# First feed-forward block of a decoder layer: both token halves taken by quarters of tokens, with one buffer and one weight moved

## The chip, the core and the metric

The kernel runs on one core of a Trainium2 chip. A core has five engines with a queue of instructions each, taken in order: TensorE (PE, with its weight loads shown as PEld), VectorE (DVE), ScalarE (ACT), GpSimd (POOL) and SyncE (SP), which issues most transfers. An engine waits at the head of its queue until the semaphores of that instruction are set; nothing behind it passes. The metric is the device time of one execution in microseconds, median of several runs.

## The reference, cut to what matters

```python
h = x + merged @ w_out
hn = rms_norm(h, norm_ffn)
return h + (jax.nn.silu(hn @ w_gate) * (hn @ w_up)) @ w_down
```

All in float32, with 1024 tokens, 1024 channels and 2816 feed-forward (FF) channels. What lies before `merged` (attention, convolution, cross-attention) isn't touched by the change.

## The kernel before

A float32 product is made of three matmuls on split operands: each operand is kept as a high part (rounded by ScalarE, L131) and a low part (the remainder, by VectorE or GpSimd, L132); `mm3` (L146) does high by high, high by low, low by high. Where a large product is made of 2 by 2 blocks, it is done in seven products instead of eight, on sums of operands ("seven", with the operands' sums in `T`).

The stage of interest lies between the output projection and the loop over FF blocks. The output projection's last matmuls (L1304) go row tile by row tile, eight tiles of 128 tokens. When one is complete, `row_done` calls `scale_h`: the sum of squares (L1197), the root by ScalarE (L138), the reciprocal (L140), and the scaled row tile `t` by VectorE (L1200), taken from a pool of four buffers, `t4`. Two row tiles make a quarter of 256 tokens. `norm_h(tp)` turns a quarter: TensorE transposes it in eight 128x128 pieces per tile (L236), four PSUM banks in all, and each bank is split into a high and a low part of `xn`, the operand of the FF products. There are two token halves of 512; quarters 0 and 2 make half 0, quarters 1 and 3 make half 1. Quarters 1 and 3 also make the sums `T` of "seven", from their own turned values and the raw values of quarters 0 and 2. These raw values are kept by ScalarE (L1231): half of them in the `fz` pool, the other half in a buffer of the `stage` pool (tag `st`), which has two buffers and is otherwise the landing place of raw weights.

FF block 0 (128 FF channels) is done plainly by `plain` (L1170), since it has no partner: gate and up products over one half at a time, 48 matmuls per product pair and quarter. For half 0 it is cut into two parts, with `norm_h(2)` between; half 1 is done in one part after `norm_h(3)`. Blocks 1 to 21 follow in a loop: `pieces(f)` loads the raw gate and up weights (SP, L1362) into `stage`, GpSimd makes the four sums (L1367 and L128), and they are split; `seven(f)` has 84 matmuls of 512 columns. After each block the activations are stored (L1146, L1152).

The order in each queue isn't the order of the code: a scheduler places instructions by priority, which falls with the place in the code, and by when it thinks operands are ready; a tile waits for a buffer of its pool. Once placed, the queues are fixed.

Of the kernel before, what the change touches and what calls it, by code (L numbers as in the profile page):

```python
# [8 lines left out]
F32 = mybir.dt.float32  # L9
F32R = mybir.dt.float32r  # L10
BF16 = mybir.dt.bfloat16
AF = mybir.ActivationFunctionType
OP = mybir.AluOpType
# [4 lines left out]
P = 128  # L18
# [3 lines left out]
KT = D // P  # L22
# [17 lines left out]
def hybrid_layer_kernel(  # L40
# [4 lines left out]
    nc = tc.nc  # L45
    x, mem, out = x[0], mem[0], out[0]
    w_in, w_mem_kv, w_out = w_in[0], w_mem_kv[0], w_out[0]
    w_gate, w_up, w_down = w_gate[0], w_up[0], w_down[0]
# [5 lines left out]
    stage = ctx.enter_context(tc.tile_pool(name="stage", bufs=2))  # L54
# [12 lines left out]
    def nm(s):  # L67
        count[0] += 1
        return f"{s}_{count[0]}"

    def slab(shape, dt=F32R):
        return slabs.tile([P] + shape, dt, tag="slab", name=nm("slab"))
# [13 lines left out]
    def t4(shape, dt=F32):  # L86
        return t4p.tile([P] + shape, dt, tag="t4", name=nm("t4"))

    def t2(shape, dt=F32, p=P):
        return t2p.tile([p] + shape, dt, tag="t2", name=nm("t2"))  # L90
# [8 lines left out]
    def bank(shape, dt=F32, p=P, at=None):  # L99
        if at is None:  # L100
            turn[1] += 1
            at = order[turn[1] % len(order)]
        return psp[at].tile([p] + shape, dt, tag=f"ps{at}", name=nm("ps"))

    def fbank(shape, dt=F32, p=P):
        return pfp.tile([p] + shape, dt, tag="pf", name=nm("pf"))

    def anybank(shape, dt=F32, p=P):
        turn[2] += 1
        j = turn[2] % 8  # L110
        return fbank(shape, dt, p) if j == 7 else bank(shape, dt, p, order[j])
# [15 lines left out]
    def sub(eng, o, a, b):  # L127
        eng.tensor_tensor(o, a, b, op=OP.subtract)  # L128
# [16 lines left out]
    def mm(o, a, b, start, stop):  # L145
        m = nc.tensor.matmul(o, a, b, start=start, stop=stop)  # L146
        n = 1
        for d in o.shape[1:]:
            n *= d
        products.append((m.ins, n if a.dtype == F32R else 4 * n))  # L150
        return m

    def mm3(o, ah, al, bh, bl, start, stop):
        first = mm(o, ah, bh, start, False)
        mm(o, ah, bl, False, False)
        mm(o, al, bh, False, stop)
        return first
# [86 lines left out]
    def xn(hl, k, half, a=0, b=512):  # L244
        return XN[half][k // 2][:, hl, k % 2, a:b]
# [20 lines left out]
    def unit(src, shape, alloc=wslab, eng=None, load=False, after=None):  # L266
        if alloc is fslab:
            st = fstp.tile([P] + shape, F32, tag="fst", name=nm("fst"))
        else:
            st = stage.tile([P] + shape, F32, tag="st", name=nm("st"))  # L270
        ld = nc.sync.dma_start(st, src)
        w = alloc([2] + shape)
        m, _ = split(w[:, 0], w[:, 1], st, eng)
        if after is not None:
            follow(m, after, "weights' cast behind attention's")
        return (w, ld.ins) if load else w

    def col_unit(w, c0, n=P, alloc=wslab, eng=None, load=False):
        return unit(w[:, c0:c0 + n].rearrange("(k p) c -> p k c", p=P), [w.shape[0] // P, n], alloc, eng,
                    load)  # L280
# [114 lines left out]
    b = bank([2 * KT])  # L395
# [11 lines left out]
    for u in range(2):  # L407
        w_ = slab([2, 2, 512])
        m, _ = split(w_[:, 0], w_[:, 1], raw_w[u])
# [20 lines left out]
    b = bank([4, TAPS + 3])  # L430
# [5 lines left out]
    b = bank([2, 16])  # L436
# [33 lines left out]
    for ct in range(4):  # L470
# [6 lines left out]
        for half in range(2):  # L477
            pg = chan_proj(wag, half)
# [10 lines left out]
    st = stage.tile([P, KT, 24], F32, tag="st", name=nm("st"))  # L489
# [14 lines left out]
    b = bank([NT, 24])  # L504
# [83 lines left out]
    for hp in range(2):  # L588
# [7 lines left out]
        b = bank([2, 256])  # L596
# [419 lines left out]
    with low(FILL):  # L1016
# [3 lines left out]
        for n_, h_ in halves:  # L1020
            b_, d_ = (2, 0, 1)[n_ // KT], n_ % KT
            if h_ == 0:
                ws[n_] = col_unit(w_in, C_GM + b_ * D + d_ * P, alloc=fslab,
                                  eng=nc.vector if n_ < N_EARLY else nc.gpsimd)
            w = ws[n_]
            ps = fbank([512])
            for k in range(KT):
                first = mm3(ps, w[:, 0, k, :], w[:, 1, k, :], xn(0, k, h_), xn(1, k, h_), k == 0, k == KT - 1)
# [70 lines left out]
    for n_, (br, wt) in enumerate(branches):  # L1099
        ins = nxt  # L1100
        for dp in range(4):
            w = unit(wt[0, :, dp * 256:(dp + 1) * 256].rearrange("(k p) c -> p k c", p=P), [4, 256],
                     alloc=anyslab if n_ else fslab if dp < 2 else wslab,
                     after=wcasts[-3] if n_ == 0 and dp > 1 else None)
# [4 lines left out]
            for d_ in (2 * dp, 2 * dp + 1):  # L1109
# [6 lines left out]
                for half in range(2):  # L1116
# [7 lines left out]
                    a = acc[dp][:, d_ % 2, half * 512:(half + 1) * 512]  # L1124
# [20 lines left out]
    def emit_act(f, half, a):  # L1145
        nc.sync.dma_start(ad[f][:, half * 512:(half + 1) * 512], a)  # L1146

    def left_low(f, a0, a1):

        s_ = t2([512])  # L1150
        sub(nc.gpsimd, s_, a0, a1)
        nc.sync.dma_start(ads[2, f], s_)  # L1152
# [14 lines left out]
    def gate_up(f):  # L1167
        return [col_unit(w, f * P, alloc=anyslab) for w in (w_gate, w_up)]

    def plain(f, half, w, parts=1, between=None):  # L1170
        pg, pu = (anybank([512]) for _ in range(2))
        for q in range(parts):
            a, b = q * 512 // parts, (q + 1) * 512 // parts
            if q:
                between()
            for o, w_ in ((pg, w[0]), (pu, w[1])):
                for k in range(KT):
                    mm3(o[:, a:b], w_[:, 0, k, :], w_[:, 1, k, :], xn(0, k, half, a, b), xn(1, k, half, a, b), k == 0,
                        k == KT - 1)
        s_ = t2([512])  # L1180
        nc.scalar.activation(s_, pg, AF.Silu)
        nc.vector.tensor_tensor(s_, pu, s_, op=OP.mult)
        emit_act(f, half, s_)
        return s_

    T = [[None] * 2 for _ in range(4)]
    raw, held, last = [None, None], [[], []], []

    def sb_fz():
        return fzp.tile([P, 2, 256], F32, tag="fz", name=nm("fz"))  # L1190
# [11 lines left out]
    def norm_h(tp, at=(None, None)):  # L1202


        half, q = tp % 2, tp // 2
        c = slice(q * 256, (q + 1) * 256)
        if q == 0:
            for kp in range(4):
                XN[half][kp] = slab([2, 2, 512])

        rows_at = []

        def turned(kp):
            b = turned_pair(js[tp], kp, at=at[kp % 2])
            rows_at.append(split(XN[half][kp][:, 0, :, c], XN[half][kp][:, 1, :, c], b))
            return b

        def keep(n, j, v, c=c):
            if T[n][j] is None:
                T[n][j] = slab([2, 2, 512])  # L1220
            two = split(T[n][j][:, 0, :, c], T[n][j][:, 1, :, c], v)
            if last:
                for pair_ in last:
                    for m, behind in zip(two, pair_):
                        tc.add_manual_dep(m.ins, behind.ins.name, ORDER, reason="sums' parts behind the rows'")

        if half == 0:
            raw[0] = [sb_fz() for _ in range(2)]
            raw[1] = stage.tile([P, 2, 2, 256], F32, tag="st", name=nm("st"))
            for kp in range(4):  # L1230
                nc.scalar.copy(raw[0][kp] if kp < 2 else raw[1][:, kp - 2], turned(kp))  # L1231
            return
        if q == 1:
            rows = [turned(kp) for kp in range(4)]
            last.extend(rows_at)
            for f_ in held[0]:
                f_()
            held[0].clear()
        for j in range(2):
            r0, r1 = (rows[j], rows[j + 2]) if q == 1 else (turned(j), turned(j + 2))  # L1240
            l0, l1 = raw[0][j], raw[1][:, j]
            d0, d1, d2 = (t2([2, 256]) for _ in range(3))
            sub(nc.vector, d0, r0, l0)
            sub(nc.vector, d1, r1, d0)
            eng = nc.vector if q == 1 else nc.gpsimd
            sub(eng, d2, d1, l0)
            sub(eng, l1, l1, d1)
            keep(0, j, d0)
            later = [lambda n=n, j=j, v=v: keep(n, j, v) for n, v in ((1, d1), (2, d2))]
            held[0] += later  # L1250
            held[1].append(lambda j=j, v=l1: keep(3, j, v))
            if q == 1:
                for f_ in held[0] + held[1][j::2]:
                    f_()
                held[0].clear()
# [75 lines left out]
    w0 = [col_unit(w_gate, 0)]  # L1331
# [8 lines left out]
    for q in range(2):  # L1340
        for j in (2 * q, 2 * q + 1):
            out_product(Y, s4, ws3, False, [(0, 1, True)], [j])
            row_done(j, 0)
            if q and j == 2:
                norm_h(1, (1, 0))
        if q:
            w0.append(col_unit(w_up, 0, eng=nc.gpsimd))
        for j in (2 * q, 2 * q + 1):
            out_product(X, plain_part(1, 1), ws4, False, [(1, 0, True)], [j])
            row_done(j, 1)  # L1350
            if j == 0:
                norm_h(0, (1, 1))
    a0 = plain(0, 0, w0, 2, lambda: norm_h(2, (1, 2)))
    norm_h(3)
    left_low(0, a0, plain(0, 1, w0))


    def pieces(f):
# [63 lines left out]
    w = pieces(1)  # L1422
    for f in range(1, FF // P):
        nxt = pieces(f + 1) if f + 1 < FF // P else None
        seven(f, *w)
        w = nxt
# [145 lines left out]
```

## Time and profile before

| | us |
|---|---|
| median of 3 runs | 1675.24 (1674.58 to 1677.42) |
| profiled execution, its time | 1675.84 |
| its span, first to last instruction | 1674.1 |
| PE busy in the span | 1632.1 (97%) |
| VectorE busy | 1100.9 (66%) |
| ScalarE busy | 745.8 (45%) |
| GpSimd busy | 669.8 (40%) |

The profile is of one execution. Times in its views run from the span's start. The stage of interest lies from about 1000 to 1080 us. A "releaser" is the instruction that the waiting engine's semaphore was set by last. The chain of waits follows the work back from the last instruction; a row there is start, length, and what ran.

### The profile page before, as it was taken

To read this page: it belongs to the slowest core of one execution; us is meant where nothing else is said; L and a number is where in the kernel's file an instruction comes from. 1 tells how busy PE (TensorE), PEld (TensorE's weight loads), DVE (VectorE), ACT (ScalarE), POOL (GpSimd) and SP (SyncE) were. 2 spreads that over 40 slices of the span, in tenths; PEclk is the share of its full clock that TensorE was granted. 3 is DMA by queue.
4 is the path that set the end of the run, shared out by engine and by line. 5 is a ranking of instruction groups with operands and counts; after the bars stand their busy time and mean duration, and the time that the engine had idled before them with its cause. 6 is when DMAs were issued, how large, how long until landed. Compare 5 with 4: busy or idle time off the path is not lost.

```text
span 1674.1 us, 22598 instructions
## 1 busy us (share of the span) xinstructions
PE 1632.1 (97%) x7904; PEld 1361.8 (81%) x7904; DVE 1100.9 (66%) x1828; ACT 745.8 (45%) x1371; POOL 669.8 (40%) x565
## 2 busy tenths in 40 slices
PE   7999999999999999999999999799999999999999
PEld 6887898777878888888788887688888888888887
DVE  6389989798666565656685867664545555466665
ACT  6311354442677676665664445333223223233332
POOL 0011004561466767656125331475566766400000
PEclk9999999999999999999999999899999999999999
DMA  8453446663355556448754432333234445893763
GB/s 286 159 172 113 149 143 177 206 200 108 108 159 166 162 153 179 134 128 266 245 178 151 164 113 95 101 120 101 88 112 139 145 154 186 283 387 122 238 227 120
DMA packets 252218, 277.87 MB, mean 166 GB/s; under 512 B 24309, under 2 KB 174117, under 8 KB 250567
## 3 DMA queue, kind: packets, MB, share of 16 engines
q1 hardware_dynamic: 245190, 263.83, 49.4%
q10 hardware_dynamic: 6912, 12.59, 2.0%
q8 instruction: 62, 1.02, 0.3%
q14 instruction: 54, 0.43, 0.1%
HBM read 191.43 MB, written 84.93 MB: 165 GB/s over the span
## 4 chain that ended last, share of the span: by engine, by line
PE 63%; DVE 6%; DMA 4%; POOL 3%; issue 3%; ACT 3%; SPq 0%; DVEq 0%; POOLq 0%; ACTq 0%
PE ps L146 31%; PE pf L146 14%; PE ps L1506 11%; PE ps L1304 3%; PE ps L965 1%; PE pf L1506 1%; DMA t<-zd 1%; DVE slab L132 1%; POOL slab L1130 1%; DMA fst<-in_w_mem_out_dram 1%; POOL slab L666 1%; DMA wd<-wsl 1%; DVE slab L467 1%; PE pf L1304 0%; DVE t L1129 0%
## 5 line engine op out<-in xcount | busy, mean ns | idle before, releaser
L146 PE MATMUL ps<-slab,wsl 128*128 128x512 f32 (+2 forms) x1664 | 362.3, 376 | 3.7 <-DVE slab L132 1.7
L146 PEld LDWEIGHTS ps<-slab,wsl 128*128 128x128 f32 x1664 | 296.8, 188 | 62.1 <-DVE slab L132 1.9
L146 PE MATMUL pf<-slab,fsl 128*128 128x512 f32 x1236 | 309.8, 394 | 3.8 <-ACT fz L1033 3.5
L146 PEld LDWEIGHTS pf<-slab,fsl 128*128 128x128 f32 x1236 | 226.9, 188 | 49.5 <-ACT fz L1033 6.1
L146 PE MATMUL ps<-slab,fsl 128*128 128x512 f32 x684 | 163.4, 394 | 6.9 <-ACT fsl L131 6.8
L467 DVE SCALAR_TENSOR_TENSOR slab<-slab,cw 128x1019 f32<-128x1019 f32 (+16 forms) x120 | 166.2, 1389 | 1.4
L1402 DVE TENSOR_TENSOR t<-ps,t 128x512 f32<-128x512 f32 x130 | 89.1, 688 | 114.5 <-PE ps L146 111.5
L146 PE MATMUL ps<-slab,slab 128*128 128x512 f32 (+1 forms) x628 | 152.8, 377 | 6.2 <-POOL slab L666 3.9
L146 PEld LDWEIGHTS ps<-slab,fsl 128*128 128x128 f32 x684 | 129.0, 190 | 35.3 <-ACT fsl L131 7.4
L146 PEld LDWEIGHTS ps<-slab,slab 128*128 128x128 f32 x628 | 112.4, 188 | 30.0 <-POOL slab L666 5.7
L1506 PE MATMUL ps<-wsl 128*128 128x512 f32 x495 | 118.9, 389 | 0.0
L1506 PEld LDWEIGHTS ps<-wsl 128*128 128x128 f32 x495 | 92.9, 188 | 19.3
L132 DVE TENSOR_TENSOR wsl<-st,wsl 128x1024 fp32r<-128x1024 f32 x57 | 84.6, 1485 | 33.5 <-ACT wsl L131 26.0
L146 PE MATMUL ps<-wsl,slab 128*128 128x512 f32 (+1 forms) x480 | 99.1, 353 | 0.4 <-DVE slab L228 0.3
L131 ACT CAST wsl<-st 128x1024 fp32r<-128x1024 f32 x61 | 63.9, 1050 | 77.7 <-PE ps L146 30.2
L146 PE MATMUL ps<-slab,qt 128*128 128x384 f32 (+6 forms) x400 | 93.8, 338 | 0.5 <-DVE sm L841 0.4
L146 PE MATMUL ps<-t,slab 128*128 128x256 f32 (+1 forms) x404 | 88.5, 319 | 1.5 <-DVE t L132 1.1
L146 PEld LDWEIGHTS ps<-wsl,slab 128*128 128x128 f32 x480 | 77.6, 192 | 12.1 <-DVE slab L228 0.5
L131 ACT CAST wsl<-t 128x1024 fp32r<-128x1024 f32 x43 | 45.3, 1054 | 89.8 <-POOL t L128 36.5
L1415 POOL TENSOR_TENSOR t<-t,t 128x512 f32<-128x512 f32 x21 | 40.0, 1907 | 112.3 <-DVE t L1402 42.0
L1506 PE MATMUL ps<-fsl 128*128 128x512 f32 x330 | 80.2, 389 | 0.0
L1130 POOL TENSOR_TENSOR slab<-slab,t 128x512 f32<-128x512 f32 x32 | 47.8, 1512 | 80.9 <-DVE t L1129 80.9
(256 smaller groups left out, 2938.1 us busy)
## 6 DMA issues: line engine op xcount, KB each, us to landing
t<-in_w_down_dram SPq DMA_DIRECT2D x70, 256.0 KB, 3.7
fst<-in_w_in_dram SPq DMA_DIRECT2D x24, 512.0 KB, 4.3
zd<-fz ACTq DMA_DIRECT2D x48, 256.0 KB, 2.4
slab<-wd SPq DMA_DIRECT2D x24, 512.0 KB, 4.6
t<-zd SPq DMA_DIRECT2D x24, 512.0 KB, 3.4
st<-in_w_gate_dram SPq DMA_DIRECT2D x22, 512.0 KB, 3.7
st<-in_w_up_dram SPq DMA_DIRECT2D x22, 512.0 KB, 4.4
ad<-t SPq DMA_DIRECT2D x44, 256.0 KB, 3.1
```

The lines of the kernel that those rows point to most:

```text
L131: m = nc.scalar.copy(hi, src)
L132: return m, (eng or nc.vector).tensor_tensor(lo, src, hi.bitcast(F32), op=OP.subtract)
L146: m = nc.tensor.matmul(o, a, b, start=start, stop=stop)
L467: return nc.vector.scalar_tensor_tensor(acc[:, s:], u[:, :S - s], cw[:, ct, 30 - s:31 - s], acc[:, s:], op0=OP.mult, op1=OP.add)
L666: part = nc.gpsimd.tensor_tensor(PT[:, 1, mb], PT[:, 1, mb].bitcast(F32), PT[:, 0, mb].bitcast(F32), op=OP.subtract)
L965: nc.tensor.transpose(b[:, j - j0, h, :], tiles[h][:, j * P:(j + 1) * P], ident)
L1130: nc.gpsimd.tensor_tensor(a, a, z, op=OP.add)
L1304: nc.tensor.matmul(B[j], a_(ha, k, j), w[:, hb, k % 2, :], start=start and k == 0 and n_ == 0, stop=stop and k == 3 and n_ == 2, skip_grou ...
L1402: nc.vector.tensor_tensor(o, a_, b_, op=OP.add)
L1415: nc.gpsimd.tensor_tensor(u4, u4, c22, op=OP.mult)
L1506: nc.tensor.matmul(B[t], a_, b_, start=start and k == 0 and j == 0, stop=k == FH - 1 and j == 2, skip_group_check=True)
```

## The change

Three edits.

1. FF block 0 is no longer done half by half. `plain` is gone; `first_part(n_, half, q)` does gate (n_ = 0) or up (n_ = 1) for one quarter of 256 tokens. The quarters 0 and 1 (both halves' first parts) come first, then the turning of quarter 2, its products, the activation of half 0, the turning of quarter 3 (now through PSUM pools 1 and 2), its products, the activation of half 1.
2. The raw half that lay in `stage` lies in a buffer of `t4`, the scaled row tiles' pool.
3. The low part of block 0's up weight is made by VectorE instead of GpSimd.

```diff
-            raw[0] = [sb_fz() for _ in range(2)]
-            raw[1] = stage.tile([P, 2, 2, 256], F32, tag="st", name=nm("st"))
+            raw[0], raw[1] = [sb_fz() for _ in range(2)], t4([2, 2, 256])
...
         if q:
-            w0.append(col_unit(w_up, 0, eng=nc.gpsimd))
+            w0.append(col_unit(w_up, 0))
...
-    a0 = plain(0, 0, w0, 2, lambda: norm_h(2, (1, 2)))
-    norm_h(3)
-    left_low(0, a0, plain(0, 1, w0))
+    first = [[anybank([512]) for _ in range(2)] for _ in range(2)]
+
+    def first_part(n_, half, q):
+        a, b = q * 256, (q + 1) * 256
+        w, o = w0[n_], first[half][n_]
+        for k in range(KT):
+            mm3(o[:, a:b], w[:, 0, k, :], w[:, 1, k, :], xn(0, k, half, a, b), xn(1, k, half, a, b), k == 0,
+                k == KT - 1)
+
+    def first_act(half):
+        s_ = t2([512])
+        nc.scalar.activation(s_, first[half][0], AF.Silu)
+        nc.vector.tensor_tensor(s_, first[half][1], s_, op=OP.mult)
+        emit_act(0, half, s_)
+        return s_
+
+    for n_ in range(2):
+        for half in range(2):
+            first_part(n_, half, 0)
+    norm_h(2, (1, 2))
+    for n_ in range(2):
+        first_part(n_, 0, 1)
+    a0 = first_act(0)
+    norm_h(3, (1, 2))
+    for n_ in range(2):
+        first_part(n_, 1, 1)
+    left_low(0, a0, first_act(1))
```

The queues move as follows. Lines after the change are numbered a little differently (L1200 is L1184, L1310 is L1293, L1338 is L1321, L1362 is L1369).

SyncE, around the stores of the finished rows `hd` (1 MB each). `st_9448` and `st_9679` are block 0's raw gate and up weights, `st_9999` and `st_10001` block 1's. Before:

```order
L271 DMA st_9448<-in_w_gate_dram 128x8x128
L1338 DMA hd<-slab_9062 128x2048
L1338 DMA hd<-slab_9063 128x2048
L1338 DMA hd<-slab_9064 128x2048
L271 DMA st_9679<-in_w_up_dram 128x8x128
L1338 DMA hd<-slab_9065 128x2048
L1146 DMA ad<-t_1681_9862 128x512
L1362 DMA st_9999<-in_w_gate_dram 128x8x128
L1146 DMA ad<-t_1700_9992 128x512
L1152 DMA ads<-t_1701_9996 128x512
L1362 DMA st_10001<-in_w_up_dram 128x8x128
```

And the same place now, where block 1's weights are `st_10047` and `st_10049`, and block 2's gate is `st_10070`:

```order
L271 DMA st_9448<-in_w_gate_dram 128x8x128
L271 DMA st_9679<-in_w_up_dram 128x8x128
L1369 DMA st_10047<-in_w_gate_dram 128x8x128
L1321 DMA hd<-slab_9062 128x2048
L1321 DMA hd<-slab_9063 128x2048
L1321 DMA hd<-slab_9064 128x2048
L1369 DMA st_10049<-in_w_up_dram 128x8x128
L1321 DMA hd<-slab_9065 128x2048
L1146 DMA ad<-t_1683_9912 128x512
L1369 DMA st_10070<-in_w_gate_dram 128x8x128
```

Block 0's up weight and block 1's gate weight moved ahead of three stores of rows, and block 1's up weight ahead of the first store of activations.

VectorE, where the first quarter's low parts (`slab_9520` to `slab_9523`) stand between the row tiles' sums and scalings (`t_1637` is the fourth scaled tile, `t_1641` the fifth). Before:

```order
L1200 SCALAR_TENSOR_TENSOR t_1637_9579<-slab_9063,sm_9577,gff 128x1024
L1310 TENSOR_TENSOR slab_9064<-ps_9076,slab_9064 128x512
L132 TENSOR_TENSOR slab_9520<-ps_9527,slab_9520 128x2x256
L132 TENSOR_TENSOR slab_9521<-ps_9535,slab_9521 128x2x256
L1197 TENSOR_TENSOR sm_9596<-sm_9058 128x1
L1310 TENSOR_TENSOR slab_9064<-ps_9077,slab_9064 128x512
L140 RECIPROCAL sm_9600<-sm_9598 128x1
```

And now (`wsl_9681` is block 0's up weight, `fsl_10057` block 1's gate weight):

```order
L132 TENSOR_TENSOR slab_9520<-ps_9527,slab_9520 128x2x256
L132 TENSOR_TENSOR slab_9521<-ps_9535,slab_9521 128x2x256
L140 RECIPROCAL sm_9600<-sm_9598 128x1
L1293 TENSOR_TENSOR slab_9064<-ps_9077,slab_9064 128x512
L132 TENSOR_TENSOR wsl_9681<-st_9679,wsl_9681 128x1024
L132 TENSOR_TENSOR fsl_10057<-st_10047,fsl_10057 128x1024
L1181 TENSOR_TENSOR sm_9670<-sm_9059 128x1
L1293 TENSOR_TENSOR slab_9065<-ps_9072,slab_9065 128x512
```

Two weights' low parts came into this place, and the fourth scaled tile left it (it now stands 14 rows behind the low part of `slab_9520`, just ahead of the fifth): `t4` has four buffers, and one of them is now held for the raw half.

TensorE, at the first products of FF block 0. `ps_9729` is the bank of gate for half 0 and `ps_9730` that of up; `pf_9731` is gate for half 1; `wsl_9450` and `wsl_9681` are the gate and up weights; `slab_9604` and on are half 1's operand. Before:

```order
L146 MATMUL ps_9729<-slab_9523,wsl_9450 128x256 x5
L236 MATMUL ps_9615<-identr,t_1622_9518 128x128
L236 MATMUL ps_9615<-identr,t_1637_9579 128x128
L236 MATMUL ps_9615<-identr,t_1622_9518 128x128
L236 MATMUL ps_9615<-identr,t_1637_9579 128x128
L146 MATMUL ps_9730<-slab_9520,wsl_9681 128x256 x2
L236 MATMUL ps_9782<-identr,t_1641_9602 128x128
```

And now:

```order
L146 MATMUL ps_9729<-slab_9520,wsl_9450 128x256 x6
L146 MATMUL ps_9729<-slab_9521,wsl_9450 128x256 x6
L146 MATMUL ps_9730<-slab_9520,wsl_9681 128x256 x6
L146 MATMUL ps_9729<-slab_9522,wsl_9450 128x256
L146 MATMUL ps_9730<-slab_9521,wsl_9681 128x256 x6
```

```order
L236 MATMUL ps_9840<-identr,t_1641_9602 128x128
L146 MATMUL pf_9731<-slab_9604,wsl_9450 128x256 x6
L236 MATMUL ps_9832<-identr,t_1641_9602 128x128
L146 MATMUL pf_9731<-slab_9605,wsl_9450 128x256
L236 MATMUL ps_9832<-identr,t_1661_9676 128x128
```

Gate and up of the first quarter now run side by side, and the products of the second quarter, which were 512 columns wide together with the fourth quarter at the end, stand between the turnings of the third.

More of the change, by code (lines that the diff above doesn't have):

```diff
@@ L1168, in gate_up @@
         return [col_unit(w, f * P, alloc=anyslab) for w in (w_gate, w_up)]
[L1170 to L1184, printed above, removed]
     T = [[None] * 2 for _ in range(4)]
```

## The prediction

> **What bounds the kernel now.** The page comes first: TensorE is busy 97% of the span, so only where it isn't can an edit of this kind gain.
>
> ```profile
> PE 1632.1 (97%) x7904; PEld 1361.8 (81%) x7904; DVE 1100.9 (66%) x1828; ACT 745.8 (45%) x1371; POOL 669.8 (40%) x565
> PE   7999999999999999999999999799999999999999
> PEclk9999999999999999999999999899999999999999
> ```
>
> Of the 40 slices only the first and the one at 1046 to 1088 us are below 9, the latter at a lower granted clock too. The windows of that stage show it closer (columns: stretch, its length, busy time of PE, PEld, DVE, ACT, POOL, granted clock, DMA share, GB/s):
>
> ```profile
> 1015.00:1020.00 5.00, 4.95 (x40) 4.60 (x38) 3.72 (x10) 3.54 (x9) 0.00 (x0) 1.00 0.48 190
> 1020.00:1025.00 5.00, 3.07 (x22) 2.69 (x23) 5.00 (x4) 2.98 (x6) 2.35 (x1) 1.00 0.13 52
> 1025.00:1030.00 5.00, 2.89 (x23) 2.48 (x23) 5.00 (x10) 1.65 (x3) 2.88 (x2) 1.00 0.00 0
> ...
> 1045.00:1050.00 5.00, 2.84 (x13) 2.02 (x11) 5.00 (x10) 3.38 (x6) 0.00 (x0) 1.00 0.00 0
> 1050.00:1055.00 5.00, 0.39 (x1) 0.40 (x2) 5.00 (x9) 2.61 (x5) 0.00 (x0) 0.67 0.36 105
> 1055.00:1060.00 5.00, 5.00 (x15) 3.68 (x15) 2.59 (x4) 0.59 (x2) 3.33 (x1) 0.64 0.23 84
> 1060.00:1065.00 5.00, 3.04 (x13) 1.87 (x12) 1.39 (x2) 1.10 (x2) 1.93 (x2) 1.00 0.44 126
> 1065.00:1070.00 5.00, 5.00 (x15) 3.89 (x16) 2.07 (x3) 3.01 (x4) 3.56 (x3) 0.66 0.38 110
> ```
>
> Two stretches have VectorE full and TensorE not (1020 to 1030, 1045 to 1055), and twice the clock falls to two thirds behind a pause. The waits of PE, for 990 to 1080 us, name the releasers:
>
> ```profile
> PE ps L146 <- ACT fsl L131: 6.8, 1, 6.8
> PE ps L146 <- DVE slab L132: 1.7, 1, 1.7
> PE ps L146 <- POOL wsl L132: 1.4, 1, 1.4
> PE pf L146 <- ACT u L131: 1.4, 1, 1.4
> PE ps L146 <- ACT wsl L131: 0.6, 1, 0.6
> PE pf L146 <- DVE u L132: 0.6, 1, 0.6
> PE ps L236 <- DVE t L128: 0.4, 1, 0.4
> ```
>
> They add up to 12.9 us. The longest ends with the cast of block 1's gate weight, which the timeline follows back to a load issued only at 1049.87, when the raw half had left its buffer of `stage`; the up weight came later still:
>
> ```profile
> 1049.87 0.38 SPq L1362 DMA_DIRECT2D st<-in_w_gate_dram  x1
> 1053.51 1.05 ACT L131 CAST fsl<-st 128x1024 fp32r<-128x1024 f32 x1
> 1054.61 7.64 PE L146 MATMUL ps<-slab,fsl 128*128 128x512 f32 x24 [6.77 <-ACT fsl L131]
> 1059.19 0.38 SPq L1362 DMA_DIRECT2D st<-in_w_up_dram  x1
> 1064.94 4.14 PE L146 MATMUL pf<-slab,u 128*128 128x512 f32 x10 [0.58 <-DVE u L132]
> 1068.92 5.68 PE L146 MATMUL ps<-slab,fsl 128*128 128x512 f32 x24
> ```
>
> **The bound of the gain.** The chain of waits (start, length, what) gives the prices of TensorE's work:
>
> ```profile
> 1028.90 3.13 PE ps L146 x24
> 1033.77 1.20 PE ps L236 x11
> 1034.97 2.98 PE pf L146 x13
> 1069.08 10.96 PE ps L146 x48
> ```
>
> A 256-column matmul costs 0.130 us, a transpose 0.109, a 512-column matmul 0.228. From 1015.4, where FF block 0 starts, to 1080.0, where block 1 ends (the last row: 1069.08 + 10.96), before runs 96 narrow and 48 wide matmuls, 40 transposes and block 1's 84 wide ones: 12.5 + 11.0 + 4.4 + 19.2 = 47.1 of 64.6 us. The other 17.5 are the 12.9 of waits and the slow clock: 24 matmuls took 7.64 for 5.5, and of the 12 on `u` the last 10 took 4.14 for 2.3, together 4.0.
>
> After the change half 1 is done in quarters: 48 wide matmuls become 96 narrow ones, 12.5 for 11.0, **+1.5 us**. Six transposes of the second quarter move from ahead of block 0 to behind its start, so it starts at 1014.9 with 46. In all 25.0 + 5.0 + 19.2 = 49.2 us: with no wait block 1 would end at 1064.1, a gain of 15.9.
>
> The Trainium skill, "TensorE: Matmul & The Clock Gate", under "Wait — 56ns, not 53.3ns?", gives the spacing of warm matmuls as columns by 2.4 GHz plus 2.5 ns, an estimate of 109 ns for 256 columns and 216 for 512, so that halving the columns would cost next to nothing and the gain be 1.4 us larger. The rows above have 130 ns, and the sum goes by them.
>
> **What goes.** The wait of 6.8 goes: block 1's gate weight now lands in the `stage` buffer that block 0's gate leaves, and its load stands ahead of the rows' stores. That buffer and the one for block 0's up weight come free with the first two of these rows; the others are the up weight's load before, and its cast:
>
> ```profile
> 991.07 2.39 POOL L132 TENSOR_TENSOR fsl<-st,fsl 128x1024 fp32r<-128x1024 f32 x1 [6.07 <-ACT fsl L131]
> 992.38 2.17 DVE L132 TENSOR_TENSOR wsl<-st,wsl 128x1024 fp32r<-128x1024 f32 x1 [0.44 <-ACT wsl L131]
> 1009.89 0.38 SPq L271 DMA_DIRECT2D st<-in_w_up_dram  x1
> 1019.44 1.05 ACT L131 CAST wsl<-st 128x1024 fp32r<-128x1024 f32 x1
> ```
>
> So the loads go out at 993.5 and 994.6 instead of 1009.9 and 1049.9. From issue to cast the slowest of the stage's loads took under 10 us (1009.89 to 1019.44, while rows were stored), so both lie ready by 1005. The 1.4 and 0.6 for block 0's up weight go too: its high part is cast at about 1008.2 (behind the casts of the first two banks), the low part by VectorE at about 1009.5, when TensorE still has the output projection. Gone with GpSimd's part is what it did to VectorE:
>
> ```profile
> 1012.96 2.48 DVE L1200 SCALAR_TENSOR_TENSOR t<-slab,sm,gff 128x1024 f32<-128x1024 f32 x2
> 1020.62 2.35 POOL L132 TENSOR_TENSOR wsl<-st,wsl 128x1024 fp32r<-128x1024 f32 x1 [27.16 <-ACT wsl L131]
> 1020.78 4.47 DVE L1200 SCALAR_TENSOR_TENSOR t<-slab,sm,gff 128x1024 f32<-128x1024 f32 x2
> ```
>
> Two scalings took 2.48 alone and 4.47 beside it: 2.0 us of VectorE's queue.
>
> **What stays, and what is new.** VectorE's queue sets the pace until about 1030. Its 128x512 operations follow at 0.60 (three in 1.87), scalings at 1.20:
>
> ```profile
> 1020.87 1.20 DVE t L1200
> 1026.97 1.87 DVE L132 TENSOR_TENSOR slab<-ps,slab 128x512 fp32r<-128x512 f32 x3
> 1018.93 0.02 issue
> ```
>
> Laid out by hand along the new queues: the two weights' low parts end at 1012.5 (the second waits for ScalarE's cast, which waits for the last output matmul on the old buffer, some 0.6 us; behind it stand row sums which TensorE needs only at 1018). The fourth and fifth scalings, late for want of a `t4` buffer, end at 1018.1 and 1019.3; TensorE meanwhile has 48 narrow matmuls of quarter 0, until 1021.0, so they cost nothing. Then it does the transposes of the second quarter, and four waits come, each on a row of VectorE's queue: the cast of the third bank, behind `t` of L128, 0.7; the cast of the first bank of quarter 2, 0.3; the PSUM bank that the next L128 frees behind two scalings and two low parts, 1.1 (VectorE 1026.85, TensorE 1025.8); the low part of `slab_9605`, two rows further, 0.7. From there TensorE has 60 narrow matmuls at a stretch, over 7 us, and VectorE goes ahead. The last scaling waits for a `t4` buffer until the last transposes of quarter 2 (1035.7), but 23 matmuls lie between those and its use, 3.0 us for 1.3.
>
> The second heap is the sums `T`: some 26 operations of VectorE (0.60 each) from 1044.4, with the four sums of block 1's weights by GpSimd beside them, which wait for `t4` buffers until quarter 3 is turned (1043.2). TensorE has 10 matmuls of block 1 and the rest of half 1 until 1050.5. The price of GpSimd beside VectorE shows in one row of before: 1.25 us of work took 3.33 beside VectorE's operations on SBUF operands.
>
> ```profile
> 1055.40 3.33 POOL L128 TENSOR_TENSOR t<-t,t 128x512 f32<-128x512 f32 x1 [21.76 <-DVE t L1182]
> ```
>
> I take it that the two alternate: VectorE loses about 3.2 us (2.6 times 1.25), and TensorE waits 1.6 at the first product on `slab_9629` and 0.5 for the bank of quarter 3, **2.1**. The ends are 0 (no collision) and 6.5 (VectorE keeps the lock while its operations follow each other, as in this row; rival 1). Beside that, some twenty hand-offs between engines at up to 0.05 (the row "issue"): 1.0.
>
> The Trainium skill, "SBUF — State Buffer", "SBUF: two separate sides", says that VectorE with two SBUF operands and GpSimd share a port pair under a lock that whoever starts first holds for a whole instruction. The rows at 1020.6 agree (the scaling ran 3.3 us); who is next when both queue, the page leaves open, and that is the 2.1 against 6.5.
>
> **Sum.** 15.9 − 0.7 − 0.3 − 1.1 − 0.7 − 2.1 − 1.0 = **10.0 us**. Behind block 1 the queues are the same but for names from block 5 on. Block 2's up weight stands on SP behind the last store of block 0's activations; by the same layout its low part ends at 1074.1 and is used at 1075.0, so it is hidden by a margin of 0.9. The profiled execution took 1675.84 for a span of 1674.1; less 10.0 that is 1665.8, and the median of the runs stands 0.6 below that execution: **1665.2**.
>
> **The rivals.**
> 1. *VectorE keeps the lock.* Then GpSimd's second and third sum come at 1045.7 and 1050.6 and the fourth after 1054, the casts of block 1's sums behind them; TensorE waits 2.5 and 3.4 instead of 1.6 and 0.5, and a pause of that kind halves the clock for some matmuls, 2.0 as at 1054.61. Gain 10.0 − 3.8 − 2.0 = 4.2: **1671.0**. For it: the row at 1055.40. Against: elsewhere its next operation waited in turn, as in the row below, 1.1 us longer than alone while a GpSimd sum ran. Chance 0.15.
>
> ```profile
> 1092.02 2.31 DVE L132 TENSOR_TENSOR slab<-t,slab 128x1024 fp32r<-128x1024 f32 x1
> ```
>
> 2. *No collision, or less.* GpSimd's four sums fit into VectorE's operations on PSUM: gain 12.1, and without hand-offs 13: **1662.2**. Chance 0.17.
> 3. *VectorE becomes the bound through the whole stage.* GpSimd has nine operations there; if each costs VectorE its full 1.25 and TensorE follows one to one, that is 11.3 instead of 3.2, a gain of 1.9: **1673.3**, no change. Against: four of the nine stand beside VectorE's reads of PSUM, where before shows them at their bare length. Chance 0.08.
> 4. *Slower: the weights' low parts at the head of VectorE's queue.* `fsl_10057` waits for its load ahead of the row sums and every scaling. It costs nothing up to an end at 1014.9 (1012.5 and 2.4 of slack), then one to one; the whole gain is gone when it ends at 1024.9, that is when the load lands after 1022. Behind the rows' stores at twice the 9.55 us that a load took there (landing 1029) it would be 6.6 late beyond that: **1681.8**. Against: the load is issued ahead of the stores. Chance 0.05.
>
> That the raw half's new place makes the rows wait (five tiles for four buffers) is in the sum; that the change doesn't do what it says would leave the gate weight's load at 1049.9, and the queue of SP excludes it.
>
> **How the numbers follow.** The forecast has 0.55. A measurement of this kernel can tell 0.2% (3.35 us) from no change, so faster is below 1671.9: 0.55 + 0.15 + 0.17 = 0.87; same 0.08; slower 0.05. The range reaches from rival 2 to rival 1, with half a microsecond to a whole on each side for the layout by hand: 1661.2 to 1671.5, which holds 0.85.
>
> **What would show it.** Windows of 1015 to 1080: PE near 5.00 from 1015 to 1023 and from 1030 to 1050, the two gaps at 1023 to 1028 and at about 1051, the granted clock at 1.00 throughout, block 2 from about 1070. The load of block 1's gate weight at 994 to 995. GpSimd's first operation in the stage only near 1027. Wrong would be: a wait of PE over 3 us, a clock below 0.9, low parts of weights on VectorE that start after 1015, or PE waiting for block 2's `wsl`.

## The result, and the profile after

| | before | after |
|---|---|---|
| median, us | 1676.33 (1674.58 to 1678.26, 4 runs) | 1664.10 (1662.73 to 1664.77, 4 runs) |
| ratio after to before, 95% interval | | 0.9926 [0.9909, 0.9943] |
| profiled execution, its time | 1675.84 | 1664.77 |
| its span | 1674.1 | 1663.0 |

The change makes the kernel 0.6 to 0.9% faster. The forecast was 1665.2, the time is 1664.1. The page of after has no slice below 9 behind the first, and 48 matmuls more, as two narrow ones take the place of one wide one:

```profile
PE 1630.5 (98%) x7952; PEld 1363.2 (82%) x7952; DVE 1103.2 (66%) x1829; ACT 746.5 (45%) x1371; POOL 669.7 (40%) x564
PE   7999999999999999999999999999999999999999
PEclk9999999999999999999999999999999999999999
```

The windows of the stage (columns as in the prediction: stretch, length, busy time of PE, PEld, DVE, ACT, POOL, granted clock, DMA share, GB/s):

```profile
1020.00:1025.00 5.00, 3.91 (x31) 3.44 (x30) 4.09 (x5) 3.52 (x7) 0.00 (x0) 1.00 0.01 2
1025.00:1030.00 5.00, 3.87 (x30) 3.45 (x30) 5.00 (x10) 1.98 (x4) 2.85 (x2) 1.00 0.00 0
...
1045.00:1050.00 5.00, 4.10 (x31) 3.48 (x29) 5.00 (x7) 3.85 (x7) 2.19 (x2) 1.00 0.29 84
1050.00:1055.00 5.00, 4.15 (x12) 3.00 (x13) 5.00 (x8) 2.39 (x4) 0.00 (x0) 0.73 0.08 24
1055.00:1060.00 5.00, 5.00 (x22) 4.13 (x21) 5.00 (x8) 2.04 (x4) 0.00 (x0) 0.93 0.00 0
```

The two gaps stand where they were forecast, at 1023 to 1028 and at 1050; TensorE does 3.9 of 5 us in the first where before had 3.0. What was not forecast is the clock: 0.73 and 0.93 behind the second gap. The waits of PE in 990 to 1085 us:

```profile
PE ps L146 <- DVE slab L132: 1.2, 1, 1.2
PE pf L146 <- ACT slab L131: 0.7, 1, 0.7
PE ps L236 <- DVE t L128: 0.7, 1, 0.7
PE ps L146 <- DVE t L128: 0.6, 1, 0.6
PE pf L146 <- DVE slab L132: 0.5, 1, 0.5
PE ps L146 <- ACT slab L131: 0.3, 1, 0.3
```

They are the six of the forecast, 4.0 us in all for 12.9 before, and none of them is for a weight. Of the loads, in SP's timeline (block 0's up weight, block 1's gate and up weight), the first two went out when it said:

```profile
992.76 0.38 SPq L271 DMA_DIRECT2D st<-in_w_up_dram  x1
993.84 0.37 SPq L1369 DMA_DIRECT2D st<-in_w_gate_dram  x1
1009.87 0.38 SPq L1369 DMA_DIRECT2D st<-in_w_up_dram  x1
```

Of the 11.1 us between the two spans, 0.7 had been won ahead of the stage: the six matmuls of the output projection that start at 985.62 in before start at 984.88 in after. The change doesn't touch what runs there, and in a second profile of after they start at 984.57, in a span of 1662.7: the lead is scatter. The stage itself gave 10.4, by the second profile 10.35.

### The profile page after: what moved, and what is told of

Read it like the earlier page. It is cut to its first block, busy times and chain, and to the rows that moved or that the text cites. A ratio compares the mean times of both kernels' runs of the same rounds, so it can differ in the third digit from the quotient of the medians.

```text
span 1663.0 us, 22705 instructions
## 1 busy us (share of the span) xinstructions
PE 1630.5 (98%) x7952; PEld 1363.2 (82%) x7952; DVE 1103.2 (66%) x1829; ACT 746.5 (45%) x1371; POOL 669.7 (40%) x564
## 4 chain that ended last, share of the span: by engine, by line
PE 71%; DVE 4%; POOL 2%; issue 2%; ACT 2%; DMA 1%; SPq 0%; DVEq 0%; POOLq 0%; ACTq 0%
PE ps L146 37%; PE pf L146 15%; PE ps L1513 11%; PE ps L1287 4%; PE ps L965 2%; PE pf L1513 1%; DVE slab L467 1%; POOL slab L666 1%; PE pf L1287 1%; POOL t L643 0%; ACT t L637 0%; DMA wd<-wsl 0%; POOL t L132 0%; PE ps L951 0%; DVE t L132 0%
## 5 line engine op out<-in xcount | busy, mean ns | idle before, releaser
L131 ACT CAST wsl<-st 128x1024 fp32r<-128x1024 f32 x61 | 64.0, 1050 | 75.7 <-PE ps L146 30.3
L131 ACT CAST wsl<-t 128x1024 fp32r<-128x1024 f32 x43 | 45.3, 1054 | 87.6 <-POOL t L128 28.7
```

What stands on the lines that cost most here:

```text
L131: m = nc.scalar.copy(hi, src)
```

## The experiments

### The three edits apart

Six kernels hold the other combinations of the three edits. The diffs are against the kernel before, and for those that take one edit back, against the kernel after.

**Edit 2 alone.**

```diff
-            raw[0] = [sb_fz() for _ in range(2)]
-            raw[1] = stage.tile([P, 2, 2, 256], F32, tag="st", name=nm("st"))
+            raw[0], raw[1] = [sb_fz() for _ in range(2)], t4([2, 2, 256])
```

> The kernel before with edit 2 alone (the raw half in a buffer of t4). Theory A, mine: the early load carries the gain. The gate load of block 1 goes out at 994 to 996, the wait of 6.8 us on its cast is gone, so are the waits on u (1.4 and 0.6), and most of the slow clock behind them; what is left is a pause at the sums T. Gain 7 to 11 us, 1665 to 1669. Theory B: the order by quarters carries it, since it gives TensorE work under VectorE's full stretches. Then this kernel gains less than 4: above 1672.

**Edit 3 alone.**

```diff
-            w0.append(col_unit(w_up, 0, eng=nc.gpsimd))
+            w0.append(col_unit(w_up, 0))
```

> The kernel before with edit 3 alone (the up weight's low part by VectorE). Theory A: the loads stay where they were (block 1's gate at about 1049), so that what TensorE wins at the first products it waits longer on that weight: gain 0 to 2 us, 1674 to 1676.5. Theory C: GpSimd beside VectorE's scalings is what held the stage up, and the gain is 4 us or more: below 1672.

**Edit 1 alone** (the kernel after, with the lines of edits 2 and 3 as before).

```diff
-            raw[0], raw[1] = [sb_fz() for _ in range(2)], t4([2, 2, 256])
+            raw[0] = [sb_fz() for _ in range(2)]
+            raw[1] = stage.tile([P, 2, 2, 256], F32, tag="st", name=nm("st"))
...
-            w0.append(col_unit(w_up, 0))
+            w0.append(col_unit(w_up, 0, eng=nc.gpsimd))
```

> The kernel after with edits 2 and 3 undone (order by quarters alone). Theory A: the gate load of block 1 is still issued at about 1049 and TensorE, which has done the second quarter's products by then, waits 6 to 9 us on its cast: gain 0 to 3, 1673 to 1676.5. Theory B: gain 6 or more, below 1670.

**Without edit 1** (the kernel before, with edits 2 and 3).

```diff
-    for n_ in range(2):
-        for half in range(2):
-            first_part(n_, half, 0)
...
+    a0 = plain(0, 0, w0, 2, lambda: norm_h(2, (1, 2)))
+    norm_h(3)
+    left_low(0, a0, plain(0, 1, w0))
```

> The kernel after with edit 1 undone: half 1 in wide products behind the fourth quarter, raw half in t4, up weight by VectorE. Theory A: the loads are early, 48 narrow matmuls fewer win 1.5 us, and the products missing between the turnings cost about as much in waits at VectorE's casts: 1663.5 to 1668. Theory B: the order was the main thing, and 6 us or more are lost against the kernel after: above 1670.

**Without edit 2.**

```diff
-            raw[0], raw[1] = [sb_fz() for _ in range(2)], t4([2, 2, 256])
+            raw[0] = [sb_fz() for _ in range(2)]
+            raw[1] = stage.tile([P, 2, 2, 256], F32, tag="st", name=nm("st"))
```

> The kernel after with edit 2 undone (raw half in the stage pool again). Theory A: block 1's gate load is issued only when that buffer is left, at about 1045 to 1050, TensorE waits 5 to 9 us for its cast, and a slow clock follows: 1671 to 1676. Theory B (the order by quarters carries the gain): below 1668.

**Without edit 3.**

```diff
-            w0.append(col_unit(w_up, 0))
+            w0.append(col_unit(w_up, 0, eng=nc.gpsimd))
```

> The kernel after with edit 3 undone (the up weight's low part by GpSimd). The loads are early, so GpSimd makes it at about 1008 to 1011, ahead of the scalings: theory A expects no difference, 1663.3 to 1665.3. Theory C (GpSimd's part was what held VectorE) expects 3 us or more, above 1667.

Measured, with the kernel after once more from a later run:

| edits | median, us | ratio to before, 95% interval |
|---|---|---|
| 1 | 1675.49 | 0.9998 [0.9990, 1.0007] |
| 3 | 1674.57 | 0.9991 [0.9982, 1.0000] |
| 1, 3 | 1675.51 | 1.0000 [0.9991, 1.0009] |
| 2 | 1665.33 | 0.9932 [0.9920, 0.9945] |
| 2, 3 | 1665.28 | 0.9935 [0.9923, 0.9948] |
| 1, 2 | 1664.59 | 0.9935 [0.9923, 0.9948] |
| 1, 2, 3 | 1664.10 | 0.9926 [0.9909, 0.9943] |
| 1, 2, 3 again | 1663.41 | 0.9931 [0.9918, 0.9945] |

Every kernel with edit 2 is 10 to 12 us faster; those without it lie within 0.1% of before. Edits 1 and 3 are worth nothing that these runs can measure, alone or beside edit 2; something like 1 us for edit 1 would be hidden in the scatter. Theory A (the early load carries the gain) had the time right in all six, B (the order by quarters does) and C (GpSimd's part does) in none where they were asked; without edit 1 the time is 1665.28, inside A's 1663.5 to 1668.

Why the order by quarters brings nothing shows in the timeline of edit 2 alone. These are a row of SP and two of PE:

```profile
994.78 0.37 SPq L1361 DMA_DIRECT2D st<-in_w_gate_dram  x1
```

```profile
1029.16 5.11 PE L146 MATMUL ps<-slab,wsl 128*128 128x256 f32 x24 [1.22 <-DVE slab L132]
...
1036.92 3.01 PE L146 MATMUL ps<-slab,fsl 128*128 128x512 f32 x12 [0.68 <-ACT t L1230]
```

With block 1's gate weight there early, the scheduler put 12 of block 1's own matmuls between the turnings. The kernel has work for TensorE's gaps from block 1 and needs none from the second quarter. It waits 4.4 us in the stage, after 4.0, and saves the 1.5 of the narrow matmuls. Most of what it saves went into the clock, which was slow here for two windows of 3.4 us and in after for one: the 24 narrow matmuls in the first row took 5.11 for the 3.13 of before. From the start of block 0 (1015.09) to the end of block 1 (1070.0, by the spans) it took 54.9 us, after 54.7.

Edit 3 alone shows the loads where they were and TensorE waiting at them. The first two rows are waits of PE, the others issues of block 1's weights:

```profile
PE ps L146 <- ACT fsl L131: 6.5, 2, 5.6
PE ps L146 <- DVE wsl L132: 1.0, 1, 1.0
```

```profile
1048.55 0.38 SPq L1362 DMA_DIRECT2D st<-in_w_gate_dram  x1
1057.86 0.38 SPq L1362 DMA_DIRECT2D st<-in_w_up_dram  x1
```

Block 0's up weight is late by its load, not by GpSimd: a wait of 1.0 stays, with VectorE as the releaser. And with edits 1 and 2 GpSimd does the part at 1008.93 in 2.41 us, ahead of the fourth scaling; VectorE starts it at 1008.63 in after. So it was the early load that took GpSimd's work out of VectorE's way, not the change of engine.

### Which of the two loads

In before the up weight of block 1 is loaded 9 us behind the gate weight. Two kernels separate the wait that the profile names (for the gate weight) from that load. The first fills the wait of 6.8 us with 28 matmuls, whose results the next product overwrites; the loads don't move.

```diff
-    def product(w, o):
+    def product(w, o, fill=0):
         ps = anybank([512])
+        for _ in range(fill):
+            m = nc.tensor.matmul(ps, w0[0][:, 0, 0, :], xn(0, 0, 0), start=True, stop=True)
...
-        nc.scalar.copy(p1, product(wt(A, 0), xb(0, 0)))
+        nc.scalar.copy(p1, product(wt(A, 0), xb(0, 0), 28 if f == 1 else 0))
```

> The kernel before with 28 matmuls more, whose results the product behind them overwrites, placed in the wait of 6.8 us for block 1's gate weight (28 x 0.228 = 6.4). Nothing else moves. Both theories expect the granted clock at 1.00 from 1048 to 1058 instead of 0.67 and 0.64. If the slow clock was a cost of its own there, block 1 ends 3.4 us earlier: 1672 to 1673. If the up weight's load (issued at 1059.19) bounds what follows, the won time turns into a longer wait on u (2.0 us before, then 4 to 5.5): 1674.5 to 1676.5.

PE's timeline (L1391 are the fillers) and two windows of it:

```profile
1047.79 6.51 PE L1391 MATMUL ps<-slab,wsl 128*128 128x512 f32 x28
...
1056.57 4.81 PE L146 MATMUL ps<-slab,fsl 128*128 128x512 f32 x20 [0.64 <-DVE fsl L132]
1063.75 0.82 PE L146 MATMUL pf<-slab,u 128*128 128x512 f32 x2 [2.37 <-ACT u L131]
```

```profile
1050.00:1055.00 5.00, 4.57 (x20) 3.49 (x20) 5.00 (x9) 2.50 (x5) 0.00 (x0) 1.00 0.37 105
1055.00:1060.00 5.00, 4.37 (x19) 3.28 (x19) 2.72 (x4) 1.31 (x3) 3.34 (x1) 1.00 0.21 78
```

The clock stays at 1.00 in both windows, and the time is 1676.30 (ratio 1.0003 [0.9994, 1.0012]). Part of the 2.1 us that the clock won went into a wait of 0.64 for the gate weight's low part, which the slow matmuls had covered; the 24 matmuls end at 1061.4, in before at 1062.2 (the first row below). What was won there went into the wait for the cast of `u`, 2.4 us for 1.4. Both waits on `u` together are 2.9 for 2.0, less than the 4 to 5.5 expected. The first product on `u` starts where it did in before (these rows are of before):

```profile
1057.46 4.78 PE L146 MATMUL ps<-slab,fsl 128*128 128x512 f32 x18
1063.63 0.73 PE L146 MATMUL pf<-slab,u 128*128 128x512 f32 x2 [1.38 <-ACT u L131]
```

It can't start earlier, since its load is issued at 1059.2 and the cast follows the landing. So the slow clock at 1051 to 1059 cost before nothing of its own. The second slow stretch, behind the wait for `u`, is there with the fillers too. One more window was slow in this profile, at 1023.28, and shorter waits behind it took that up: the last product of block 0 ends where it did in before.

The second kernel is after with block 1's up weight alone back behind the store of block 0's activations:

```diff
         for w in (w_gate, w_up):
...
+        if f == 1:
+            tc.add_manual_dep(m.ins, stored[0].ins.name, ORDER, reason="block 1's up weight behind block 0's stores")
```

> The kernel after, with block 1's up weight alone loaded where it was before, behind the store of block 0's difference of activations; the gate weight stays early. Theory A in the form that the fillers left of it (both loads are late in before, and the up weight's, the later one, sets when block 1 ends): TensorE does the 24 matmuls on the gate weight early, then waits for u until about 1064 to 1067 with 60 matmuls to go, and the gain is gone: 1672 to 1677. Theory A as forecast (the wait on the gate weight's cast is the main term): most of the gain stays, 1664 to 1669.

```profile
1059.55 0.38 SPq L1371 DMA_DIRECT2D st<-in_w_up_dram  x1
```

```profile
1050.91 3.00 PE L146 MATMUL ps<-slab,fsl 128*128 128x512 f32 x12 [0.45 <-DVE t L128]
1064.02 5.51 PE L146 MATMUL pf<-slab,u 128*128 128x512 f32 x12 [10.11 <-ACT u L131]
```

The time is 1674.35 us (0.9993 [0.9984, 1.0002]). With the gate weight early and the up weight late, the whole gain is gone: one wait of 10.1 us for `u`. So the later load sets the end of block 1. In before it stood behind the gate weight's load, which waited for the raw half's buffer, and behind the stores of block 0's activations in SP's queue; edit 2 moved both loads ahead of all that.

### The second gap

GpSimd's four sums of block 1's weights run beside VectorE's sums `T`. This kernel gives them the third `wsl` buffer, so that they needn't wait for `t4`, and queues them behind quarter 1's last subtraction:

```diff
-        s12, s34 = t4([2, 4, P]), t4([2, 4, P])
+        if f == 1:
+            both = wslab([2, 2, 4, P], F32)
+            s12, s34 = both[:, 0], both[:, 1]
+        else:
+            s12, s34 = t4([2, 4, P]), t4([2, 4, P])
...
+        if f == 1:
+            for i_ in (m, m2):
+                tc.add_manual_dep(i_.ins, raws[1].ins.name, ORDER, reason="block 1's sums behind quarter 1's")
```

> The kernel after, with block 1's four sums by GpSimd in the third wsl buffer instead of two of t4, queued behind quarter 1's last subtraction: they run at about 1034 to 1040, where VectorE has pauses, instead of 1041 to 1047 beside the sums T. If the alternation of GpSimd and VectorE (some 2.7 us of VectorE's queue) makes the two pauses of TensorE at the sums T (1.2 and 0.6) and these the slow clock (0.73 and 0.93, 1.9 us): all of it goes, the clock is 1.00 throughout, 1660 to 1661.5. Rival: VectorE's own 26 operations bound TensorE there, and the pauses stay within half a microsecond: 1663 to 1664.5.

1662.77 us (0.9923 [0.9910, 0.9935]). The two rows below are the same two operations of VectorE, in after beside GpSimd's sums and here without them:

```profile
1042.60 3.52 DVE L132 TENSOR_TENSOR slab<-t,slab 128x512 fp32r<-128x512 f32 x2
```

```profile
1043.66 1.28 DVE L132 TENSOR_TENSOR slab<-t,slab 128x512 fp32r<-128x512 f32 x2
```

GpSimd cost VectorE 2.2 us at that place, and 0.5 at the next two operations of this kind (1.79 for 1.29, at 1046.64 in after). Both pauses at the sums are gone, and the clock is 1.00 through the stage, as the first theory has it. But two new waits came, for a copy of the raw half and for a low part, since the cast and the low part of the first sum now stand ahead of them:

```profile
1038.85 0.66 PE L236 MATMUL ps<-identr,t 128*128 128x128 f32 x4 [0.86 <-ACT t L1214]
...
1040.33 0.86 PE L146 MATMUL pf<-slab,wsl 128*128 128x256 f32 x5 [0.48 <-DVE slab L132]
```

The time lies between the two theories, and its interval overlaps that of after.

Two more kernels go on from there. One also moves the scaling of quarter 3's first row tile behind quarter 1's subtractions:

```diff
+        if t == 6:
+            tc.add_manual_dep(m.ins, subs[-1].ins.name, ORDER, reason="quarter 3's first row behind quarter 1's sums")
```

> As the run with the early sums, and the scaling of the first row tile of quarter 3 (1.2 us) queued behind quarter 1's subtractions, ahead of nothing that TensorE waits for. If VectorE's queue makes the pauses at 1023 to 1028, those for t of L128 (0.7) and for the low part of slab_9605 (0.5) go or shrink: a further 0.6 to 1.1 us, 1659 to 1661. Rival: the pauses there are hand-offs that the scaling doesn't matter to, no difference from the run with the early sums.

1662.96 us. The waits of the first gap shrank as expected, from 0.6 to 0.3 (for `t`) and from 0.5 to 0.24 (for the low part). They came back at the next scaling, which now stood beside GpSimd's sums, and the time is the rival's, that of the run with the early sums:

```profile
1034.90 2.26 DVE L1184 SCALAR_TENSOR_TENSOR t<-slab,sm,gff 128x1024 f32<-128x1024 f32 x1 [2.46 <-PE ps L236]
```

It took 1.29 in after, and TensorE waited 0.6 for it. The other puts the first sum's cast and low part behind the rows that they had delayed:

```diff
+        if f == 1:
+            for i_, behind in ((m[0], kept[-1]), (m[1], last[0][1])):
+                tc.add_manual_dep(i_.ins, behind.ins.name, ORDER, reason="block 1's first sum behind quarter 3's rows")
```

> The run with the early sums, and the cast of block 1's first sum queued on ScalarE behind the last copy of the raw half, its low part on VectorE behind quarter 3's first low part. If the two new pauses of that run (0.86 for the copy, 0.48 for the low part) came from those two rows standing ahead, they go: 1661 to 1662, the clock 1.00 or one window down. Rival: the low part in its new place delays the sums T and the pauses come back there: 1662.5 to 1664.

1663.90 us (0.9929 [0.9916, 0.9941]). The wait of 0.86 for the copy went, but one of 0.43 for a cast came behind it; that of 0.48 became 0.22, and new ones of 0.2 and 0.3 came further on. The sum of the waits went from 3.5 to 3.3. The rival had the time. Beside it ran the kernel after, unchanged:

> The kernel after once more, beside the run with the held sum and on the same chip: 1663.5 to 1664.8. If the clock falls by whole windows of 3.41 us on a grid that has nothing to do with the program, the stage shows a drop at another place than the first profile, or none, with the same waits.

1663.41 us, 0.1 below what was expected, with the same six waits as in the first profile. The clock was expected to fall at another place or not at all; it fell at nearly the same place, from 1051.97 to 1055.38 for 1052.26 to 1055.67. None of the three variants can be told from after. What is left of the stage are short waits for VectorE and ScalarE, and in these three runs moving one row made another one late.

## Why the prediction was right, point by point

**The bound and the sum.** From the start of block 0 to the end of block 1 the forecast has 49.2 us of work and 5.9 of losses, 55.1. After has block 0's start at 1014.16, which with the 0.7 won ahead is the forecast's 1014.9; block 1's end, by the spans, is 1080.0 − 11.1 = 1068.9. That makes 54.7, so 5.5 of losses. (The 1015.4 that the prediction gives for the start of block 0 in before is 0.2 early, as its first matmul starts at 1015.62; the 1014.9 from which the sum goes on is right.)

| | forecast, us | after, us |
|---|---|---|
| first gap, four waits | 2.8 | 2.2 |
| sums `T`, two waits | 2.1 | 1.8 |
| hand-offs | 1.0 | −0.2 (what is left over) |
| slow clock | 0 | 1.7 (half of one window of 3.41) |

The gain in the stage was 10.4 for 10.0. Three sizes were off and nearly cancelled: the waits by 0.9, the hand-offs by 1.2 (the prices, taken from consecutive rows of PE, presumably hold them already), the clock by 1.7. That they cancel is luck. The other 0.7 of the difference lie ahead of the stage and are scatter.

**What goes.** The wait of 6.8 went, and the loads went out at 992.8 and 993.8 for a forecast of 993.5 and 994.6. The reading of it was incomplete: it took the wait for the gate weight and the slow clock of 4.0 for costs that add up. The fillers show that the first part of the slow clock (7.64 for 5.5) was free, and the late up weight that the wait for the gate weight was free as well: the up weight's load held block 1 behind both. The total came out because it was taken as a bound from TensorE's work, not as a sum of the waits.

**Block 0's up weight.** The 1.4 and 0.6 went with the load. The 2.0 us of VectorE's queue that the text gave to the change of engine belong to the early load too: with GpSimd the time is the same (1664.59).

**The order by quarters.** Its price, 1.5 us, was in the sum. Its return was not worked out by itself, and the runs show none: 1665.28 without it, 1664.10 and 1663.41 with it, intervals that overlap.

**GpSimd beside VectorE.** The forecast took alternation, 3.2 us of VectorE's queue, over keeping the lock. It was 2.7 (the 2.2 and 0.5 above), and GpSimd's four sums ended at 1047.3 instead of running past 1054: rival 1 was wrong. So was rival 2, since the collision came, and rival 3, since beside GpSimd's operations at 1025.9 to 1033.6 VectorE's kept their bare length (four in 2.48 at 1026.30). The weight's low part at the head of VectorE's queue (rival 4) ended at 1011.2, 3.7 us ahead of the point from which it would cost.

**The clock.** "1.00 throughout" was wrong, and a clock below 0.9, which the prediction names as a sign of being wrong, came: 0.73. The slow clock is a term that the sum had at nothing. The other signs did not come. The forecast counted a slow clock only behind the longer pauses of rival 1 (2.5 and 3.4); 1.2 and 0.6 were enough.

## What to carry to other kernels

A staging buffer that is lent to something else delays not only the next load into it, but every transfer that stands behind that load in the queue; look for the last of them, because the wait that the profile names first may hide a longer one. A gain is better bounded by the work of the busiest engine than added up from its waits, since waits and a slow clock in front of a late transfer cost nothing by themselves: filling one is a cheap test. And where a scheduler fills gaps by itself, bring its operands in early before you cut work into smaller pieces for it.

## What the runs showed of the hardware

**The clock falls in whole windows on a grid of its own.** These are windows of 3.41 us of the kernel before, laid so that the edges of the slow stretches are their edges (the granted clock is the third figure from the right):

```profile
1048.32:1051.73 3.41, 0.00 (x0) 0.00 (x0) 3.41 (x7) 0.62 (x1) 0.00 (x0) 1.00 0.12 32
1051.73:1055.14 3.41, 0.53 (x1) 0.50 (x2) 3.41 (x6) 2.75 (x5) 0.00 (x0) 0.50 0.40 122
1055.14:1058.56 3.42, 3.42 (x9) 2.40 (x8) 2.45 (x4) 0.46 (x1) 3.16 (x1) 0.50 0.20 77
1058.56:1061.97 3.41, 3.41 (x16) 2.69 (x15) 0.00 (x0) 0.00 (x0) 0.17 (x1) 1.00 0.63 186
1061.97:1065.38 3.41, 1.45 (x6) 0.69 (x5) 1.77 (x2) 1.10 (x2) 2.31 (x2) 1.00 0.15 44
1065.38:1068.80 3.42, 3.42 (x10) 2.67 (x9) 0.53 (x2) 1.81 (x3) 3.17 (x3) 0.50 0.41 119
```

Each window's clock follows from how busy TensorE was in the window ahead: 0.00, 0.53 and 1.45 of 3.41 us give 0.50 in the next, 3.41 gives 1.00. In all eleven profiles in which it fell in this stage, it fell for one, two or three times 3.41 to 3.42 us, and where it fell at two or three places of one profile, they lie whole multiples of 3.41 apart (1051.73 and 1065.38 are four). In after the window ahead of the slow one was half busy:

```profile
1048.85:1052.26 3.41, 1.66 (x7) 0.92 (x6) 3.41 (x7) 2.77 (x6) 0.00 (x0) 1.00 0.47 139
1052.26:1055.68 3.42, 3.42 (x10) 2.67 (x9) 3.42 (x5) 0.78 (x1) 0.00 (x0) 0.50 0.00 0
```

In this stage, over these profiles, every window at the full clock with 1.67 us or less was followed by a slow one, none with 2.00 or more; of those between, 1.93 and 1.95 were, 1.90 was not. So a pause of some 1.5 us can cost 1.7 more, by where the grid lies. Both kernels have such a pause at 380 us, where they run the same work. In before it left a window 1.49 busy and the next was slow, in after 1.69 and the next was not (first row before, second after; so 1.69 belongs to the open range as well):

```profile
379.31:382.72 3.41, 1.49 (x9) 1.29 (x10) 3.41 (x4) 0.00 (x0) 2.87 (x3) 1.00 0.65 201
379.83:383.25 3.42, 1.69 (x11) 1.55 (x12) 3.42 (x5) 0.27 (x1) 2.86 (x2) 1.00 0.46 137
```

The kernel with edits 1 and 2 has TensorE's queue and nearly the waits of after, and there the clock stayed at 1.00 behind the second gap and fell behind the first, from 1028.26 to 1031.67:

```profile
1024.84:1028.26 3.42, 1.95 (x13) 1.29 (x12) 3.42 (x6) 1.66 (x3) 1.53 (x1) 1.00 0.01 2
1028.26:1031.67 3.41, 3.41 (x18) 3.41 (x17) 3.41 (x7) 1.21 (x2) 1.52 (x3) 0.50 0.02 5
```

Part of the scatter between runs of one kernel goes with this: the five of after's second run with mean clocks of 0.999, 0.999 and 0.999 took 1662.33, 1662.74 and 1663.41 us, those with 0.998 and 0.996 took 1664.39 and 1667.39, and one slow window is 0.001 of the span. The Trainium skill, "TensorE: Matmul & The Clock Gate", under "What's actually happening", has a window of 3413 ns that runs freely, and two states; the rows agree with both. It puts the slow state behind at least one idle window; here a window that was half busy did it, and the measurement decides.

**Who is next when GpSimd and VectorE both work on SBUF.** When both had operations on SBUF operands in their queues, the two alternated at the sums `T`: VectorE took 3.52 us for two operations of 0.64, and GpSimd's sums 1.3 to 1.74 each. Later GpSimd alone was held up, as in before (2.88 in the last row below, 3.33 in before, for about 1.3 alone):

```profile
1043.82 1.74 POOL L128 TENSOR_TENSOR t<-t,st 128x512 f32<-128x512 f32 x1
1045.64 1.64 POOL L128 TENSOR_TENSOR t<-st,t 128x512 f32<-128x512 f32 x1
1060.93 2.88 POOL L128 TENSOR_TENSOR t<-t,t 128x512 f32<-128x512 f32 x1 [13.66 <-DVE t L1348]
```

What decides between the two ways was not tried, and no run here shows it.
